# A list schedule takes the order of its choices from a table: runs of instructions with a turn of their own, in a four-layer model on one core

## The chip, the cores and the metric

The kernel runs on one core of a Trainium2 chip. Its time is the device time of one execution in microseconds (us), and lower is better. The engines are named as in the profile: PE (TensorE matmul) and PEld (its weight load), DVE (VectorE), ACT (ScalarE), POOL (GpSimd) and SP (SyncE, which here only issues DMAs).

## The reference

A stack of four layers works on 512 tokens of 1024 features, in float32. Each layer is a mixer and a gated feed-forward block, each with an RMS norm in front and a residual behind; the four mixers differ.

```python
for i in range(DEPTH):                       # 4
    hn = rmsnorm(h, norm_mix[i])
    if t == 0:   m = rwkv7_mix(hn, ...)      # 16 heads, a state of 64x64 per head, a scan over the tokens
    elif t == 1: m = swa_sink_mix(hn, ...)   # attention in a window of 128, 16 query and 2 key heads
    elif t == 2: m = sgu_chunk_mix(hn, ...)  # gelu, a gate that mixes tokens in chunks of 128
    else:        m = gla_mix(hn, ...)        # gated linear attention, 4 heads
    h = h + m
    gate, up = split(rmsnorm(h, norm_ffn[i]) @ ffn_w_in[i])
    h = h + (silu(gate) * up) @ ffn_w_out[i] # hidden size 2816
return rmsnorm(h, norm_final)
```

## The kernel before

Every product in float32 is made of three products in the faster float32r form: both operands are split into a rounded part and a remainder, and `mm3` (L584) issues high times high, high times low and low times high into one PSUM bank. A weight tile goes through three steps: a DMA brings it as `wraw`, ACT copies its rounded part to `whi`, and DVE subtracts that and leaves the remainder in `wlo`. There are 8 `wraw`, 4 `whi` and 4 `wlo` buffers, and 8 PSUM banks, which the program calls `ps`.

The feed-forward blocks and several projections use seven products in place of eight (`seven`, L833, a Strassen-like scheme). Some of its weight operands are sums: the first quarter comes by a DMA that SP issues, and a second DMA, issued by POOL, adds another quarter to the same `wraw` buffer. That buffer is added to only after ACT and DVE have read it for the product before. A feed-forward block has six hidden parts and three output parts, each of seven products. The seven are named m1, m2, m5, m3, m6, m7, m4 in order. The last three are accumulated in the same two banks one after the other, and DVE reads the banks between them: into `slot` tiles in the hidden half (`hidden`, L909), into the residual `h` in the output half (`out_steps`, L819). So m7 can write a bank only when DVE has read m6 from it.

The first mixer has a serial part (`rwkv_chain`, L1325): for each chunk of 64 tokens PE multiplies, ACT copies a result to `vu`, PE multiplies with that (operand `tok`), and DVE makes the next state `st`. While one group of heads goes through its chain, `ahead` (L1105) prepares the next one, with many small steps on ACT (`ew`, `et`) and DVE. The second mixer (`swa`, L1432) projects the queries (`project`, eight tiles of 24 matmuls of 128x512 each), and computes scores for blocks of 128 tokens (`attend`, L1486): matmuls of 128x256 and 128x128 into a bank, which DVE then reads with a mask.

What sets the order of the work is not the order of the program text. All calls are recorded first as 18309 `Op` objects (`record`, L226; the profile gives L234, the line of that helper, for nearly all instructions), with their number `i`, their dependencies, and a cost from a formula (`price`, L264). Then `run` (L290) is a list scheduler: it keeps for each engine the ready instructions in a list sorted by `i`, walks through it, and takes the first one that can start, unless a later one can start over 200 ns (`SLACK`) sooner. Over all engines the candidate that starts first is issued. Only instructions up to 700 (`WINDOW`) behind the first unfinished one are looked at. Each engine then executes its instructions in that order, and waits where one is not ready.

Where the scheduler's own clock sees PE idle for over 450 ns (`GAP`), `keep_warm` (L398) puts in products of the identity matrix with itself, which compute nothing that is used ("fills"; `products`, L493, L496 in the profile), to hold the clock that the hardware grants to TensorE. `ahead_of_cold` (L422) adds some where too little work lies in the last stretch.

Of the kernel before, what the change touches and what calls it, by code (L numbers as in the profile page):

```python
# [28 lines left out]
TABLES = {AF.Exp: "exp", AF.Ln: "ln", AF.Sigmoid: "sigmoid", AF.Tanh: "tanh", AF.Silu: "silu", AF.Gelu: "gelu", AF.Sin: "sin"}  # L29
ALSO = {"exp": ("tanh",), "sigmoid": ("tanh",), "silu": ("sin", "tanh"), "gelu": ("tanh",)}  # L30
ORDER = 1
EARLY = (("pa", 1), ("iv", 4), ("ew", 4))
LATE = (("qk", 4), ("pr", 1), ("et", 11), ("mt", 6), ("tok", 3), ("wu", 2), ("vu", 4), ("out", 5))
VECS = ("norm_mix", "rw_mu", "rw_w0", "rw_a0", "rw_k_k", "rw_k_a", "rw_r_k", "rw_gn_g", "rw_gn_b", "norm_ffn", "sw_b_qkv", "sg_b_u", "gla_b_a",
# [141 lines left out]


class Op:
    __slots__ = ("i", "eng", "call", "deps", "outs", "wait", "cost", "lat", "table", "bufs", "ready", "end", "done", "columns", "form")


class Engine:
# [7 lines left out]
class Program:  # L190
# [99 lines left out]
    def run(self):  # L290
        ops, n = self.ops, len(self.ops)
        for op in ops:
            op.wait = len(op.deps)
            for d in op.deps:
                d.outs.append(op)
            for b in op.bufs:
                b.left += 1
# [3 lines left out]
        dma, table, work = 0.0, None, {}  # L301
        self.work = work
        avail = {e: [] for e in now}
        head, limit = 0, 0
        order = 0
        while order < n:
# [2 lines left out]
            new = min(n, head + self.WINDOW)  # L309
            for op in ops[limit:new]:  # L310
                if op.wait == 0:
                    bisect.insort(avail[op.eng], (op.i, op))
            limit = max(limit, new)
            best = None
            for e, lst in avail.items():
                cand, floor = None, None
                for i, op in lst:
                    s = max(now[e], op.ready)
                    ok = True
                    for b in op.bufs:  # L320
                        if b.held:
                            continue
                        sl = b.pool.slots[b.name]
                        if not sl.may(b, head) or b.psum and b.span[0] > head and len(sl.free) <= self.FREE and not self.soon(b, head):
                            ok = False
                            break
                        s = max(s, min(sl.free) + self.SEM)
                    if not ok:
                        continue
                    if op.table and op.table != table and not (table and op.table in ALSO.get(table, ())):  # L330
                        s += 1300.0
                    if floor is None or s < floor - self.SLACK:
                        if floor is None or s < floor:
                            floor = s
                        cand = (s, i, op)
                    elif s < floor:
                        floor = s
                    if floor <= now[e]:
                        break
                if cand:  # L340

                    if best is None or cand[0] < best[0]:
                        best = cand + (e,)
            if best is None:
                raise RuntimeError("no instruction can go on at %d of %d: %s" % (order, n, [(e, len(l)) for e, l in avail.items()]))
            s, i, op, e = best
            if e == "PE" and self.warm and op.ready > 0.0:
                now["PE"] = self.keep_warm(now["PE"], s, work)
                if now["PE"] > s or self.ahead_of_cold(now, s, op, work):
                    continue  # L350
            avail[e].remove((i, op))
            if op.table and op.table != table and not (table and op.table in ALSO.get(table, ())):
                table = op.table
            cost = op.cost
# [11 lines left out]
            end = s + cost  # L366
# [17 lines left out]
            for o in op.outs:  # L384
                raw = o.deps[op]
                if o.eng == e and e == "PE" or o.eng == "":
                    t = end
                elif o.eng == e:
                    t = (fin if raw else end) if op.lat != 2000.0 else fin
                else:  # L390
                    t = fin if raw else (end + self.SEM if op.lat != 2000.0 else fin)
                o.ready = max(o.ready, t)
                o.wait -= 1
                if o.wait == 0 and o.i < limit:
                    bisect.insort(avail[o.eng], (o.i, o))
        self.time = max(now.values())

    def keep_warm(self, now, s, work):  # L398
# [1624 lines left out]
```

## Time and profile before

| What | Value |
|---|---|
| Time, median of 3 runs | 2528.71 us (2522.41 to 2529.03) |
| Time of the profiled execution | 2518.66 us |
| Its span, first to last instruction | 2516.9 us |
| Mean granted TensorE clock | 0.995 |
| Instructions | 37778, of them 14254 matmul records |
| Read from HBM | 393.95 MB |

The span is what the profile shows; the execution's own time is 1.8 us longer. The profiled execution is 10 us faster than the median of the runs. A float32 matmul leaves two records in the trace, a float32r matmul or a transpose one. The ends of matmuls are modelled, and neighbours overlap in the records. The stages in the trace, by the place of their matmuls: first mixer to 500 us, feed-forward 500 to 840, second mixer 840 to 1009, feed-forward to 1348, third mixer to 1624, feed-forward to 1961, fourth mixer to 2168, feed-forward to the end.

### The profile page before, as it was taken

What the parts mean: (1) busy time and instruction counts of PE and PEld (TensorE: products, weight loads), DVE (VectorE), ACT (ScalarE), POOL (GpSimd) and SP (SyncE); (2) the same over time, 40 slices, a digit from 0 to 9 for tenths busy, and PEclk for the clock granted to TensorE, in tenths of its full rate; (3) what the DMA queues carried; (4) which work ended last, traced back from release to release, by engine and by line L of the source; (5) the groups of instructions that cost most, each with busy time, mean ns of one, the idle gap of its engine ahead of it and who ended that gap; (6) DMA issues with size and microseconds to landing.
All of it is one profiled execution on the core that took longest, in us unless ns stands there. A gap on an engine that the chain in (4) does not pass through costs nothing.

```text
span 2516.9 us, 37778 instructions
## 1 busy us (share of the span) xinstructions
PE 2451.4 (97%) x14254; PEld 2013.8 (80%) x14254; DVE 1935.5 (77%) x3051; ACT 1398.1 (56%) x2269; POOL 406.9 (16%) x456
## 2 busy tenths in 40 slices
PE   9999999999999999999999999999999999999998
PEld 8577778998878766988787788898878888888786
DVE  7684886688778874887779877887768878976868
ACT  4544454465646456756466444665546756755555
POOL 0000000022122232121211300122111221121111
PEclk9999999999999999999999999999999999999999
DMA  5220002389897422898987836699888775889885
GB/s 170 67 69 10 10 4 69 115 199 230 214 229 175 119 85 51 187 219 226 206 212 174 241 101 155 138 216 234 207 214 188 174 184 128 184 205 225 218 200 120
DMA packets 128631, 400.88 MB, mean 159 GB/s; under 512 B 14384, under 2 KB 21040, under 8 KB 128448
## 3 DMA queue, kind: packets, MB, share of 16 engines
q0 software_dynamic: 50688, 171.99, 38.6%
q1 hardware_dynamic: 77760, 226.47, 27.1%
q8 instruction: 112, 1.84, 0.3%
q14 instruction: 71, 0.58, 0.1%
HBM read 393.95 MB, written 2.10 MB: 157 GB/s over the span
## 4 chain that ended last, share of the span: by engine, by line
PE 68%; DVE 11%; DMA 8%; issue 6%; ACT 5%; POOL 1%; SPq 0%; DVEq 0%; POOLq 0%; ACTq 0%
PE ps L234 68%; DMA wraw<-ffn_w_b 4%; DVE slot L234 4%; DVE wlo L234 2%; DMA wraw<-ffn_o_a 2%; ACT slot L234 2%; ACT whi L234 2%; DVE h L234 1%; DVE et L234 1%; DMA wraw<-ffn_o_b 1%; POOL wraw L234 1%; PE ps L496 1%; DVE left L234 1%; POOL slot L234 0%; DVE mt L234 0%
## 5 line engine op out<-in xcount | busy, mean ns | idle before, releaser
L234 PE MATMUL ps<-whi,slot 128*128 128x512 f32 (+1 forms) x4960 | 1529.3, 384 | 17.7 <-DVE slot L234 11.2
L234 PEld LDWEIGHTS ps<-whi,slot 128*128 128x128 f32 x4960 | 921.6, 188 | 196.7 <-issue 20.0
L234 ACT CAST whi<-wraw 128x1024 fp32r<-128x1024 f32 (+3 forms) x680 | 674.9, 997 | 636.5 <-PE ps L234 446.1
L234 DVE TENSOR_TENSOR wlo<-wraw,whi 128x1024 fp32r<-128x1024 f32 (+2 forms) x680 | 786.7, 1165 | 258.4 <-ACT whi L234 255.7
L234 PE MATMUL ps<-wlo,slot 128*128 128x512 f32 (+1 forms) x2480 | 948.1, 383 | 4.3 <-DVE wlo L234 4.0
L234 PEld LDWEIGHTS ps<-wlo,slot 128*128 128x128 f32 x2480 | 466.2, 188 | 85.5 <-DVE wlo L234 8.7
L234 PE MATMUL ps<-slot,whi 128*128 128x512 f32 (+3 forms) x976 | 277.8, 367 | 1.8 <-ACT slot L234 0.9
L234 DVE TENSOR_TENSOR slot<-ps,slot 128x512 f32<-128x512 f32 (+2 forms) x269 | 157.5, 607 | 73.5 <-PE ps L234 57.7
L234 PEld LDWEIGHTS ps<-slot,whi 128*128 128x128 f32 (+2 forms) x976 | 170.4, 184 | 47.2 <-DVE slot L234 8.8
L234 POOL DMA_DIRECT2D wraw<-ffn_w_a x128 | 110.4, 863 | 514.1 <-DVE wlo L234 434.6
L234 DVE TENSOR_TENSOR slot<-left,slot 128x512 fp32r<-128x512 f32 (+1 forms) x250 | 161.0, 662 | 36.3 <-ACT slot L234 30.7
L234 DVE TENSOR_TENSOR h<-h,ps 128x512 f32<-128x512 f32 x240 | 159.2, 684 | 32.1 <-PE ps L234 29.9
L234 PE MATMUL ps<-slot,wlo 128*128 128x512 f32 (+3 forms) x488 | 177.2, 363 | 0.0
L234 ACT CAST slot<-left 128x512 fp32r<-128x512 f32 (+1 forms) x250 | 145.3, 601 | 40.8 <-PE ps L234 26.4
L234 ACT COPY slot<-ps 128x512 f32<-128x512 f32 (+1 forms) x154 | 85.2, 566 | 57.4 <-PE ps L234 54.0
L234 POOL DMA_DIRECT2D wraw<-ffn_w_b x64 | 55.5, 876 | 317.0 <-DMA wraw<-ffn_w_b 95.9
L234 PEld LDWEIGHTS ps<-slot,wlo 128*128 128x128 f32 (+2 forms) x488 | 89.7, 184 | 16.6 <-issue 2.9
L234 POOL DMA_DIRECT2D wraw<-ffn_o_a x64 | 55.2, 862 | 275.2 <-DVE wlo L234 161.6
L234 PE MATMUL ps<-ident,slot 128*128 128x128 f32 (+2 forms) x672 | 89.1, 265 | 1.7 <-DVE slot L234 1.5
L234 PEld LDWEIGHTS ps<-ident,slot 128*128 128x128 f32 (+2 forms) x672 | 69.2, 140 | 26.6 <-issue 5.7
L234 DVE TENSOR_TENSOR slot<-slot 128x512 f32<-128x512 f32 (+7 forms) x131 | 77.5, 611 | 4.2 <-ACT slot L234 2.3
L234 ACT COPY left<-ps 128x512 f32<-128x512 f32 x100 | 50.5, 556 | 53.5 <-PE ps L234 53.4
(281 smaller groups left out, 2299.7 us busy)
## 6 DMA issues: line engine op xcount, KB each, us to landing
wraw<-ffn_w_a SPq DMA_DIRECT2D x128, 512.0 KB, 6.5
wraw<-ffn_w_a POOLq DMA_DIRECT2D x128, 512.0 KB, 6.2
wraw<-ffn_o_a SPq DMA_DIRECT2D x64, 512.0 KB, 5.0
wraw<-ffn_o_a POOLq DMA_DIRECT2D x64, 512.0 KB, 7.8
wraw<-ffn_w_b SPq DMA_DIRECT2D x64, 384.0 KB, 3.6
wraw<-ffn_w_b POOLq DMA_DIRECT2D x64, 384.0 KB, 6.4
wraw<-ffn_o_b SPq DMA_DIRECT2D x16, 512.0 KB, 4.4
wraw<-ffn_o_b POOLq DMA_DIRECT2D x16, 512.0 KB, 8.0
```

What stands on the lines that cost most here:

```text
L234: op = self.add(eng.name, lambda: getattr(eng.target, what)(*map(real, args), **{k: real(a) for k, a in kw.items()}), *self.price(eng.name ...
L496: self.nc.tensor.target.matmul(t, i, i, start=True, stop=True)
```

## The change

Each instruction gets a `turn`, at first its number. A table `TURNS` of 117 rows (first number, end, shift) over all stages moves runs of instructions: their turn is their number plus the shift. The lists of ready instructions are sorted by the turn, and by the number where turns are equal. All else stays: instructions, dependencies, costs, the window of 700 (which still goes by the number), buffers and the rule of the 200 ns.

```diff
+TURNS = (
+    (0, 192, -3283), (192, 384, -2134), (384, 412, -1837), (412, 464, -482), (464, 492, -1382), (536, 588, -2292), (616, 644, 25), (696, 724, -1506),
...
+    (6688, 6717, 14279), (6722, 6751, 3372), (6751, 6758, -290), (6830, 6859, -211), (7118, 7147, 4551), (7154, 7183, -371), (7190, 7219, 12145),
...
+)
...
     def run(self):
         ops, n = self.ops, len(self.ops)
         for op in ops:
+            op.turn = op.i
+        for a, b, t in TURNS:
+            for op in ops[a:b]:
+                op.turn = op.i + t
...
-                    bisect.insort(avail[op.eng], (op.i, op))
+                    bisect.insort(avail[op.eng], (op.turn, op.i, op))
...
-                for i, op in lst:
+                for _, i, op in lst:
...
-            avail[e].remove((i, op))
+            avail[e].remove((op.turn, i, op))
...
-                    bisect.insort(avail[o.eng], (o.i, o))
+                    bisect.insort(avail[o.eng], (o.turn, o.i, o))
```

Some shifts are large: a run with +14279 is last in its list until the window of 700 stops the others, a run with -3283 is first. Others are a few dozen, which puts two neighbouring products of a feed-forward block at nearly the same turn.

The programs differ in two counts: the fills, and the loads of ACT's function tables. Of 142 fills (each a matmul of two records) 98 are left: 57 at the start in both, 43 (in 15 pieces) between 200 and 422 us of the profile of before against 22 (in 6), 10 in the second mixer against none, 14 in other places ahead of 500 us or in the third and fourth mixer against none, and 18 against 19 in the output projection of the first mixer. ACT's table loads go from 22 to 20. All other instructions are the same, in another order. The line numbers grow: L234 becomes L253, and L496 becomes L520.

Three places show how. The first is ACT in the chain of the first mixer, around 225 to 233 us of the profile of before. `vu<-ps` is the copy that the chain waits for, `out` and `tok` belong to the chain too, and `ew` and `et` to the group that is being prepared. Before:

```order
L234 COPY vu<-ps 64x256
L234 ACT_TABLE_LOAD
L234 ACTIVATE ew<-ps,vec 128x512 x4
L234 ACTIVATE et<-ew,ka_1330,vec 128x512 x2
L234 COPY out<-ps 64x256
L234 COPY tok<-ps 128x512
L234 COPY vu<-ps 64x256
```

The same two copies of the chain in the changed program:

```order
L253 COPY vu<-ps 64x256
L253 ACT_TABLE_LOAD
L253 ACTIVATE et<-ew 128x512 x3
L253 COPY out<-ps 64x256
L253 COPY tok<-ps 128x512
L253 COPY vu<-ps 64x256
```

Between one `vu` copy of the chain and the next stood six activations and now stand three; the four of `ew` have moved ahead of the chain.

The second place is PE in the second mixer, at 872 to 881 us. Matmuls of 128x256 and 128x128 are scores, those of 128x512 with `whi` or `wlo` are a projection, and those of L496 are fills. Before:

```order
L234 MATMUL ps<-slot 128x128 x4
L234 MATMUL ps<-slot 128x256 x8
L234 MATMUL ps<-slot 128x128 x2
L234 MATMUL ps<-slot 128x256 x3
L496 MATMUL ps<-ident 128x128 x2
L234 MATMUL ps<-slot 128x256
L496 MATMUL ps<-ident 128x128 x2
L234 MATMUL ps<-slot 128x256 x4
```

The same scores in the changed program:

```order
L253 MATMUL ps<-slot 128x128 x4
L253 MATMUL ps<-slot 128x256 x8
L253 MATMUL ps<-slot,whi 128x512 x2
L253 MATMUL ps<-slot,wlo 128x512
L253 MATMUL ps<-slot,whi 128x512 x2
L253 MATMUL ps<-slot,wlo 128x512
L253 MATMUL ps<-slot,whi 128x512 x2
L253 MATMUL ps<-slot,wlo 128x512
L253 MATMUL ps<-slot,whi 128x512 x2
L253 MATMUL ps<-slot 128x256 x2
```

The scores came in one lump with fills in it, and now are spread between the matmuls of a projection that has been held back.

The third place is PE in the last feed-forward block, at 2382 to 2386 us, with the numbers of the buffers. It is the step from m6 to m7 in an output half: `ps_22204` and `ps_22216` are the two banks that DVE must read in between. Before:

```order
L234 MATMUL ps_22204<-whi_22349,slot_22324 128x512
L234 MATMUL ps_22216<-whi_22349,slot_22297 128x512
L234 MATMUL ps_22216<-wlo_22366,slot_22297 128x512
L234 MATMUL ps_22216<-whi_22349,slot_22324 128x512
L234 MATMUL ps_22216<-whi_22349,slot_22297 128x512
L234 MATMUL ps_22216<-wlo_22366,slot_22297 128x512
L234 MATMUL ps_22216<-whi_22349,slot_22324 128x512
L234 MATMUL ps_22204<-whi_22370,slot_22321 128x512
```

In the changed program the two banks have the numbers 22137 and 22150, and `ps_22356` and `ps_22374` belong to the next hidden product. The first rows of the same step:

```order
L253 MATMUL ps_22137<-whi_22282,slot_22303 128x512
L253 MATMUL ps_22150<-whi_22282,slot_22230 128x512
L253 MATMUL ps_22356<-whi_22300,slot_20461 128x512
L253 MATMUL ps_22150<-wlo_22309,slot_22230 128x512
L253 MATMUL ps_22356<-wlo_22327,slot_20461 128x512
```

After thirteen more rows, the first bank is written again, in the last row here:

```order
L253 MATMUL ps_22150<-whi_22371,slot_22254 128x512
L253 MATMUL ps_22374<-whi_22300,slot_20525 128x512
L253 MATMUL ps_22356<-whi_22341,slot_20510 128x512
L253 MATMUL ps_22356<-wlo_22360,slot_20510 128x512
L253 MATMUL ps_22137<-whi_22371,slot_22254 128x512
```

Between the last write of m6 into the first bank and the first of m7 lay 6 matmuls, and now lie 21, since another product runs mixed with this one. Counted over the whole program, the matmuls of 128x512 and 128x384 in a feed-forward block change the bank that they write 1096 times before and 1917 times now.

More of the change, by code (lines that the diff above doesn't have):

```diff
@@ L178 @@
 class Op:
-    __slots__ = ("i", "eng", "call", "deps", "outs", "wait", "cost", "lat", "table", "bufs", "ready", "end", "done", "columns", "form")
+    __slots__ = ("i", "eng", "call", "deps", "outs", "wait", "cost", "lat", "table", "bufs", "ready", "end", "done", "columns", "form", "turn")
 class Engine:
@@ L292, in run @@
         for op in ops:
+            op.turn = op.i
+        for a, b, t in TURNS:
+            for op in ops[a:b]:
+                op.turn = op.i + t
+        for op in ops:
             op.wait = len(op.deps)
```

15 rows, old and new, of the table TURNS are left out of this document.

## The prediction

> **What bounds the kernel now.** I read the busy times of the engines first, then the chain that ended last, then the stages in windows of time, and last the timeline at the waits.
>
> ```profile
> span 2516.9 us, 37778 instructions
> PE 2451.4 (97%) x14254; PEld 2013.8 (80%) x14254; DVE 1935.5 (77%) x3051; ACT 1398.1 (56%) x2269; POOL 406.9 (16%) x456
> ...
> L234 PE MATMUL ps<-whi,slot 128*128 128x512 f32 (+1 forms) x4960 | 1529.3, 384 | 17.7 <-DVE slot L234 11.2
> ```
>
> TensorE is busy for 97% of the span, so by this row 65.5 us are idle. That is a lower bound for what waiting costs, since one matmul record lasts 384 ns, while in the chain below 316 of them follow each other in 71.05 us, 225 ns apiece: a gap shorter than some 160 ns is hidden behind the record's own modelled end.
>
> ```profile
> 586.68 71.05 PE ps L234 x316
> ...
> 2454.27 51.63 PE ps L234 x232
> ```
>
> The second row says where PE's work ends: at 2505.9 us, 11.0 us before the span does.
>
> The Trainium skill says the same more strongly ("Perfetto Trace Analysis", section Identifying the Most-Contended Engine): matmul busy time is a bad measure of the distance to the limit, and the busy time of the weight loads a good one. By the 80% of the PEld row there would be 503 us of room; no term below uses that, because the 225 ns pitch leaves a reordering nothing to take from a dense stretch.
>
> The stages, in the columns PE, PEld, DVE, ACT and POOL busy, granted clock (PEclk), DMA share and GB/s:
>
> ```profile
> 20.00:200.00 180.00, 176.37 (x1031) 128.24 (x1031) 137.62 (x232) 84.30 (x126) 2.05 (x8) 1.00 0.24 72
> 200.00:422.00 222.00, 210.73 (x2959) 170.39 (x2954) 163.69 (x393) 111.92 (x230) 11.21 (x18) 0.98 0.07 23
> ...
> 500.00:840.00 340.00, 335.56 (x1591) 280.53 (x1591) 278.20 (x376) 201.49 (x290) 72.19 (x80) 1.00 0.88 208
> 840.00:1009.00 169.00, 164.18 (x784) 118.21 (x783) 105.00 (x211) 90.04 (x260) 51.42 (x45) 0.97 0.25 68
> 1009.00:1348.00 339.00, 335.65 (x1598) 281.58 (x1596) 266.72 (x357) 204.48 (x300) 63.41 (x74) 1.00 0.88 209
> 1348.00:1624.00 276.00, 267.64 (x1255) 219.16 (x1254) 228.13 (x346) 137.25 (x196) 40.57 (x40) 1.00 0.65 163
> 1624.00:1961.00 337.00, 334.28 (x1597) 281.16 (x1596) 263.75 (x350) 200.29 (x288) 63.37 (x74) 1.00 0.90 208
> 1961.00:2168.00 207.00, 201.69 (x1137) 167.68 (x1136) 174.66 (x288) 132.30 (x221) 39.25 (x41) 1.00 0.73 164
> 2168.00:2517.00 349.00, 331.39 (x1560) 279.07 (x1558) 265.60 (x371) 192.60 (x271) 60.50 (x70) 0.99 0.82 191
> ```
>
> PE is the bound in every stage, and no other engine is full: DVE has 164 of 222 us in the chain of the first mixer. So the time can only fall by what PE loses to waits, to fills and to a lower clock, and only an order of work can change that. Losses stand in three kinds of places: the chain of the first mixer (200 to 422 us), the second mixer (840 to 1009), and single waits in the feed-forward blocks.
>
> **The change part by part.** No useful instruction is added or removed, so the sum goes by stage. The fills, by the groups of line 496, whole and in the two stages:
>
> ```profile
> L496 PE MATMUL ps<-ident 128*128 128x128 f32 x284 | 42.8, 303 | 3.6 <-DVE slot L234 1.9 <-POOL ident L234 1.4
> ...
> L496 PE MATMUL ps<-ident 128*128 128x128 f32 x86 | 13.8, 299 | 0.1
> ...
> L496 PE MATMUL ps<-ident 128*128 128x128 f32 x20 | 5.5, 426 | 2.1 <-DVE slot L234 1.9
> ```
>
> *First mixer, 200 to 422 us.* PE is idle for 222.00 - 210.73 = 11.3 us, fills take 13.8 us (86 records, 43 fills), and the clock of 0.98 costs 0.02 x 222 = 4.4 us: 29.5 us that are not work. How such a wait arises:
>
> ```profile
> 225.98 1.28 ACT L234 ACT_TABLE_LOAD   x1
> ...
> 227.27 2.43 ACT L234 ACTIVATE ew<-ps,vec 128x512 f32<-128x512 f32 x4
> ...
> 229.57 1.53 ACT L234 ACTIVATE et<-ew,ka,vec 128x512 f32<-128x512 f32 x2
> ...
> 229.95 0.83 PE L496 MATMUL ps<-ident 128*128 128x128 f32 x6
> ...
> 232.12 0.37 ACT L234 COPY vu<-ps 64x256 f32<-64x256 f32 x1
> ...
> 232.54 0.71 PE L234 MATMUL ps<-vu,tok 128*128 128x128 f32 x4 [1.76 <-ACT vu L234]
> ...
> 234.23 1.67 ACT L234 ACTIVATE et<-ew 128x512 f32<-128x512 f32 x3
> ```
>
> ACT works in its own order, and the copy that the chain needs stood behind six activations of the next group (2.43 + 1.53 = 3.96 us); PE did 0.83 us of fills and waited 1.76. In the first place of the new order three activations stand there, 1.67 us by the last row: ACT is free 2.3 us sooner, nearly the 2.6 us of fills and wait. That is one place. For the stretch I go by the fills that the scheduler still puts in, 22 for 43: it fills where its own clock sees PE idle, and by that clock 21 of 43 holes are gone. I let idle time, fills and lost clock shrink alike, by 21/43. Gain 29.5 x 0.49 = 14.4 us; the bounds are 0 (each fill is replaced by idling) and 29.5.
>
> *Second mixer.* Idle 169.00 - 164.18 = 4.8, fills 5.5, clock 0.03 x 169 = 5.1: 15.4 us.
>
> ```profile
> 877.47 1.08 PE L496 MATMUL ps<-ident 128*128 128x128 f32 x4 [0.82 <-DVE slot L234]
> ...
> 879.12 0.69 DVE L234 SCALAR_TENSOR_TENSOR slot<-ps,mask 128x512 f32<-128x512 f32 x1
> ```
>
> Scores come in a lump, and each bank of them must be read by DVE (0.69 us) before the next can be written. In the new order (second place) projection matmuls stand between, 24 x 0.225 = 5.4 us for each tile held back, and the fills here are none. I take two thirds, 10.3 us, and not all, because the last blocks of attention have no projection left to hide behind. Bounds 0 and 15.4.
>
> *Fills elsewhere.* 14 go and one comes, at 42.8 / 142 = 0.30 us each: 3.9 us. If nothing fills their place it is 0.
>
> *Feed-forward blocks.* Their idle time is 4.4, 3.4 and 2.7 us in the first three, and 349.00 - 331.39 - 11.0 = 6.6 in the last: 17.1 us. A clock dip adds to it:
>
> ```profile
> 235.00:250.00 15.00, 14.97 (x113) 11.75 (x112) 12.98 (x26) 4.76 (x11) 0.31 (x1) 0.81 0.07 19
> ...
> 925.00:940.00 15.00, 12.82 (x71) 9.35 (x70) 12.06 (x21) 1.73 (x2) 1.48 (x1) 0.79 0.32 83
> 2220.00:2230.00 10.00, 7.51 (x37) 6.93 (x35) 5.40 (x8) 5.03 (x8) 0.00 (x0) 0.83 0.49 138
> 2381.00:2386.00 5.00, 2.48 (x12) 1.78 (x11) 4.19 (x5) 1.93 (x3) 0.00 (x0) 1.00 0.97 278
> ```
>
> That is 0.17 x 10 = 1.7 us in the row at 2220. The two longest waits:
>
> ```profile
> 2223.56 0.44 PE L234 MATMUL ps<-whi,slot 128*128 128x384 f32 x1 [2.49 <-DVE slot L234]
> ...
> 2382.56 1.05 ACT L234 CAST whi<-wraw 128x1024 fp32r<-128x1024 f32 x1 [1.43 <-DMA wraw<-ffn_o_a]
> ...
> 2383.64 1.23 DVE L234 TENSOR_TENSOR wlo<-wraw,whi 128x1024 fp32r<-128x1024 f32 x1 [0.65 <-ACT whi L234]
> 2384.78 1.28 DVE L234 TENSOR_TENSOR h<-h,ps 128x512 f32<-128x512 f32 x2
> 2385.61 0.47 PE L234 MATMUL ps<-whi,slot 128*128 128x512 f32 x1 [2.52 <-DVE h L234]
> ```
>
> The lower four rows are one cause: weights land late, so ACT's copy and DVE's `wlo` are late, and the reading of the bank that PE waits for is queued behind that `wlo` on DVE. In the new order (third place) 21 matmuls lie between m6 and m7 where 6 lay; 15 more at 0.225 us are 3.4 us, over the 2.52. Of the 17.1 us I take two thirds, 11.4, since some steps still run unmixed, and the dip with it: 13.1 us, bounds 0 and 18.8. For the third and fourth mixer (8.4 + 5.3 us idle) I take nothing.
>
> *ACT's tables.* Two loads less spare ACT 2 x 1.28 us. It is busy for 56% of the span, and where it does hold PE up the chain's term above has it, so I count nothing more.
>
> *What is new.* Two products mixed hold two pairs of the four `whi` and `wlo` buffers, so a weight tile is prepared with less lead, and DVE's queue decides more often. The price of one miss is a `wlo` pass, 1.23 us by the row above; I take five, 6.2 us. The bounds are 0 and the rival below.
>
> Sum: 14.4 + 10.3 + 3.9 + 13.1 - 6.2 = 35.5 us. The profiled execution took 2518.66 us, 1.8 more than its span, so the changed one would take 2483 in such an execution. The runs shown have their median 10 us higher, at 2528.71; on that scale it is 2493 us. A measurement of this kernel can tell about 0.3%, 7.6 us, from no change.
>
> **The rivals.** *More goes than I take* (chance 0.10): all of the first three terms and of the feed-forward, 29.5 + 15.4 + 3.9 + 18.8 = 67.6 us, gives 2461. For it: the fills show that the scheduler sees few holes left. Against it: 17.1 us of idling in feed-forward stages had hardly a fill, so its clock doesn't see them all.
>
> *The holes stay, only empty* (0.10): a fill stands where PE has nothing ready. If the chains on ACT and DVE are as long as before, PE idles in place of the fills, and the few waits won are paid back by new ones: 2529. For it: DVE is busy for 164 of 222 us in the chain, so a copy moved forward pushes another back. Against it: the two first places put real work there, not nothing.
>
> *The clock* (0.05): fills are there to hold it, and nine of the fifteen pieces of fills between 200 and 422 us go. If each of the nine brings a dip like that at 235 us, 0.19 x 15 = 2.9 us, that is 26 us, and 2519 are left: 0.4% faster. Against it: fills stood in the dips at 235 and 925 us and did not prevent them. The Trainium skill has the rule ("TensorE: Matmul & The Clock Gate", Part 1): after an idle window of about 3.4 us the array runs at half rate. By that rule, single holes well below 3.4 us bring no dip; the trace is divided on it, with a clock of 1.00 around the wait of 2.52 us at 2385 and of 0.83 around that of 2.49 us at 2224.
>
> *Weights come late* (0.09), on the other side: the feed-forward windows have a DMA share of 0.88 to 0.90, and mixed products ask for the loads of two at once from the same 8 `wraw` buffers. Each late landing ahead of a bank's reading costs 2.5 us, as at 2224 and 2385. Seventeen of them eat the 41.7 us that the other terms give; with 20, one in 13 of the 252 products of the four blocks, the time is 2537. For it: such waits exist, and DMA is fullest there. Against it: a buffer is added to for a later product, and mixing puts more PE time between the two uses, as in the third place.
>
> **How the numbers follow.** The main case has 0.66, with 20 to 50 us gained: 2479 to 2509, 2493 the likeliest. The range goes on to the case of more at 2461 and to no change at 2529, which leaves out the late weights, half of the empty holes, and the tail beyond 2461. Faster by over 0.3%: 0.66 + 0.10 + 0.03 of the clock = 0.79; within: 0.10 + 0.02 = 0.12; slower: 0.09.
>
> **What would show it.** Right: between 200 and 422 us of before the stage takes about 14 us less and the second mixer about 10; at the m6 to m7 step of the last block no wait of 2.5 us is left; PE idle falls from 65.5 to some 45 us. Wrong: stages of the same length with PE busy lower (empty holes), a granted clock of 0.95 or less in the first mixer (clock), or feed-forward stages longer than 340 us with waits of ACT for `wraw` (late weights).

## The result and the profile after

The changed kernel takes 2466.68 us, the median of 4 runs (2461.81 to 2470.02). The kernel before, run beside it, takes 2526.2 us (4 runs, 2522.41 to 2529.03). The ratio is 0.9764, with an interval from 0.9738 to 0.979: 59.5 us less by the medians. The profiled execution of the changed kernel took 2470.02 us, near the top of its runs, and that of before was near the bottom of its own, so the two traces differ by less: 2516.9 - 2468.3 = 48.6 us of span. What follows about stages explains these 48.6 us.

The head of the page of the changed kernel, with the group of plain matmuls:

```profile
span 2468.3 us, 37524 instructions
PE 2411.1 (98%) x14166; PEld 1995.9 (81%) x14166; DVE 1930.5 (78%) x3051; ACT 1389.3 (56%) x2267; POOL 400.2 (16%) x456
...
L253 PE MATMUL ps<-whi,slot 128*128 128x512 f32 (+1 forms) x4960 | 1509.7, 385 | 13.7 <-DVE slot L253 7.4
```

PE's idle time went from 65.5 to 2468.3 - 2411.1 = 57.2 us, which is little. Its busy time fell by 40.3 us, although every useful matmul is still there. So most of the gain lies inside what the profile calls busy: fills, clock, and matmuls that follow each other more closely.

The stages of the changed kernel, in windows, with the columns of the prediction's table (PE, PEld, DVE, ACT and POOL busy, granted clock, DMA share, GB/s). The first mixer ends at 474 us, the others are at 815 to 971, 1310 to 1577 and 1921 to 2128 us, and the feed-forward blocks lie between and behind them:

```profile
20.00:200.00 180.00, 179.88 (x1065) 134.37 (x1066) 139.85 (x236) 87.90 (x132) 1.64 (x6) 1.00 0.23 74
200.00:400.00 200.00, 191.10 (x2910) 156.01 (x2906) 162.14 (x391) 103.33 (x222) 10.72 (x19) 1.00 0.09 28
...
474.00:815.00 341.00, 333.83 (x1581) 280.93 (x1579) 274.53 (x373) 198.26 (x284) 71.53 (x79) 0.99 0.87 206
815.00:971.00 156.00, 150.85 (x768) 111.50 (x767) 105.19 (x212) 90.30 (x261) 49.21 (x45) 1.00 0.26 73
971.00:1310.00 339.00, 334.77 (x1595) 283.73 (x1594) 266.02 (x357) 202.98 (x300) 62.05 (x74) 0.99 0.89 209
1310.00:1577.00 267.00, 265.47 (x1244) 218.35 (x1242) 224.50 (x345) 138.64 (x196) 38.54 (x38) 1.00 0.66 164
1577.00:1921.00 344.00, 335.09 (x1590) 281.59 (x1589) 263.43 (x350) 198.42 (x288) 62.73 (x75) 1.00 0.86 205
1921.00:2128.00 207.00, 201.44 (x1138) 167.91 (x1137) 175.89 (x291) 133.57 (x223) 40.27 (x42) 1.00 0.73 165
2128.00:2468.30 340.30, 329.03 (x1560) 277.59 (x1558) 265.27 (x370) 191.19 (x270) 60.56 (x70) 0.99 0.85 198
```

The first three mixers are shorter, and all four are at full clock; the fourth is as long as before. In the second mixer 156.00 - 150.85 = 5.15 us are idle, and there is no fill: what was 15.4 us of waits, fills and lost clock is 5.15. In the third mixer the idle time went from 8.4 to 1.5 us. The feed-forward blocks are idle longer than before: 7.2, 4.2, 8.9 and, in the last one, 340.3 - 329.0 less a tail of 10.3 us, 1.0: 21.3 us against 17.1.

What PE waited for, longest sums first (total us, times, longest us), in the changed kernel and then in before:

```profile
PE ps L253 <- DVE slot L253: 20.1, 15, 3.5
PE ps L253 <- DVE wlo L253: 4.1, 6, 1.2
PE ps L253 <- DVE h L253: 3.8, 4, 1.1
...
PE ps L253 <- ACT vu L253: 0.9, 1, 0.9
```

```profile
PE ps L234 <- DVE slot L234: 17.3, 25, 2.5
PE ps L234 <- DVE h L234: 9.6, 9, 2.5
PE ps L234 <- ACT vu L234: 4.8, 7, 1.9
```

The wait for the chain's `vu` copy is nearly gone (4.8 to 0.9 us), and so are the waits for `h`: none of them is over 1.1 us, so the 2.52 us at the step from m6 to m7 are gone. The waits for `slot` are fewer and longer; the longest, 3.5 us, is in a feed-forward block.

For every traced execution I also added up the distances from one PE record to the next by the stage to which the matmul belongs (fills go to the stage of the next useful matmul). This table is used throughout; times are in us. The tail is from the start of PE's last record to the end of the span:

| Execution | 1st mixer | FFN 1 | 2nd | FFN 2 | 3rd | FFN 3 | 4th | FFN 4 | tail | span |
|---|---|---|---|---|---|---|---|---|---|---|
| before | 497.2 | 339.6 | 170.3 | 338.0 | 276.5 | 336.4 | 207.8 | 338.1 | 11.4 | 2516.9 |
| changed | 470.3 | 342.3 | 156.8 | 338.0 | 268.0 | 344.4 | 206.2 | 330.5 | 10.3 | 2468.3 |
| e1, first mixer's rows | 469.6 | 341.7 | 177.2 | 341.9 | 274.5 | 339.6 | 209.7 | 332.5 | 11.5 | 2499.5 |
| e2, no FFN rows | 469.5 | 341.0 | 157.6 | 341.4 | 268.6 | 336.8 | 206.4 | 335.0 | 11.4 | 2469.1 |
| e3, FFN rows only | 497.3 | 341.0 | 171.0 | 337.0 | 274.0 | 343.1 | 210.9 | 330.6 | 10.2 | 2516.6 |
| e4, before, no later fills | 498.4 | 340.1 | 169.5 | 344.1 | 275.8 | 336.7 | 210.5 | 334.5 | 11.4 | 2522.5 |
| e6, second mixer's rows | 496.4 | 341.3 | 159.3 | 341.3 | 277.2 | 337.9 | 209.1 | 335.4 | 11.5 | 2510.9 |
| e7, third and fourth | 496.6 | 340.7 | 171.0 | 341.0 | 268.9 | 336.2 | 207.3 | 332.9 | 11.7 | 2507.8 |
| e8, changed, no later fills | 467.5 | 344.2 | 160.4 | 339.2 | 266.7 | 342.1 | 210.0 | 330.0 | 10.2 | 2471.6 |
| e9, changed, small adds | 469.5 | 334.0 | 156.8 | 332.1 | 266.0 | 332.3 | 204.7 | 328.3 | 10.3 | 2435.5 |
| e10, before, small adds | 496.0 | 338.6 | 168.9 | 336.5 | 273.3 | 335.2 | 206.5 | 331.5 | 11.4 | 2499.4 |
| e11, front rows only | 486.6 | 344.9 | 169.0 | 340.4 | 275.7 | 337.5 | 207.8 | 335.1 | 11.4 | 2509.8 |
| e12, changed, FFN 3 as before | 470.1 | 342.8 | 158.0 | 336.2 | 269.1 | 338.6 | 208.2 | 329.3 | 10.3 | 2464.0 |

The first mixer is the same to 2 us wherever its order is the same. A feed-forward block differs by up to 6 us from execution to execution of one order (the second one in before's order: 338.0 to 344.1). The second mixer in before's order took 168.9 to 171.0 us, but 177.2 in e1; the fourth took 206.5 to 210.9. So only the first mixer may be read from one trace, and a difference of a few us in the others only from several.

### The profile page after: what moved, and what is told of

It is laid out like the page before. It is cut to its first block, busy times and chain, and to the rows that moved or that the text cites. A ratio compares the mean times of both kernels' runs of the same rounds, so it can differ in the third digit from the quotient of the medians.

```text
span 2468.3 us, 37524 instructions
## 1 busy us (share of the span) xinstructions
PE 2411.1 (98%) x14166; PEld 1995.9 (81%) x14166; DVE 1930.5 (78%) x3051; ACT 1389.3 (56%) x2267; POOL 400.2 (16%) x456
## 4 chain that ended last, share of the span: by engine, by line
PE 71%; DMA 9%; DVE 9%; ACT 5%; issue 4%; POOL 1%; SPq 0%; DVEq 0%; POOLq 0%; ACTq 0%
PE ps L253 71%; DMA wraw<-ffn_w_a 3%; DMA wraw<-ffn_w_b 2%; DVE wlo L253 2%; ACT slot L253 2%; DVE slot L253 2%; DMA wraw<-ffn_o_a 2%; ACT whi L253 1%; DVE h L253 1%; POOL wraw L253 1%; DVE et L253 1%; DMA wraw<-sg_w_v 1%; DVE mt L253 0%; DMA wraw<-gla_w_qk 0%; POOL slot L253 0%
## 5 line engine op out<-in xcount | busy, mean ns | idle before, releaser
L253 PE MATMUL ps<-whi,slot 128*128 128x512 f32 (+1 forms) x4960 | 1509.7, 385 | 13.7 <-DVE slot L253 7.4
L253 PEld LDWEIGHTS ps<-whi,slot 128*128 128x128 f32 x4960 | 923.4, 188 | 186.2 <-DVE slot L253 14.7
L253 ACT CAST whi<-wraw 128x1024 fp32r<-128x1024 f32 (+2 forms) x680 | 673.8, 997 | 619.5 <-PE ps L253 426.6
L253 DVE TENSOR_TENSOR wlo<-wraw,whi 128x1024 fp32r<-128x1024 f32 (+2 forms) x680 | 783.7, 1161 | 237.9 <-ACT whi L253 233.8
L253 PE MATMUL ps<-wlo,slot 128*128 128x512 f32 (+1 forms) x2480 | 932.7, 383 | 4.1 <-DVE wlo L253 4.1
L253 PEld LDWEIGHTS ps<-wlo,slot 128*128 128x128 f32 x2480 | 466.8, 188 | 85.7 <-DVE wlo L253 7.9
L253 PE MATMUL ps<-slot,whi 128*128 128x512 f32 (+3 forms) x976 | 276.1, 366 | 1.8 <-ACT slot L253 0.9
L253 DVE TENSOR_TENSOR slot<-ps,slot 128x512 f32<-128x512 f32 (+2 forms) x269 | 159.0, 607 | 79.7 <-PE ps L253 70.6
L253 PEld LDWEIGHTS ps<-slot,whi 128*128 128x128 f32 (+2 forms) x976 | 170.4, 184 | 40.4 <-issue 4.5
L253 POOL DMA_DIRECT2D wraw<-ffn_w_a x128 | 111.0, 879 | 483.2 <-DVE wlo L253 339.4
L253 DVE TENSOR_TENSOR h<-h,ps 128x512 f32<-128x512 f32 x240 | 159.0, 684 | 26.6 <-PE ps L253 24.3
L253 DVE TENSOR_TENSOR slot<-left,slot 128x512 fp32r<-128x512 f32 x250 | 160.2, 662 | 23.5 <-ACT slot L253 15.4
L253 PE MATMUL ps<-slot,wlo 128*128 128x512 f32 (+3 forms) x488 | 176.5, 366 | 0.0
L253 ACT CAST slot<-left 128x512 fp32r<-128x512 f32 (+1 forms) x250 | 143.4, 601 | 29.0 <-PE ps L253 18.0
L253 ACT COPY slot<-ps 128x512 f32<-128x512 f32 (+2 forms) x154 | 85.3, 566 | 72.4 <-PE ps L253 66.0
L253 PEld LDWEIGHTS ps<-slot,wlo 128*128 128x128 f32 (+2 forms) x488 | 89.5, 184 | 18.4 <-issue 3.7
L253 POOL DMA_DIRECT2D wraw<-ffn_o_a x64 | 55.9, 873 | 297.3 <-DVE wlo L253 210.5
L253 POOL DMA_DIRECT2D wraw<-ffn_w_b x64 | 55.1, 867 | 300.2 <-DVE wlo L253 99.4
L253 PE MATMUL ps<-ident,slot 128*128 128x128 f32 (+2 forms) x672 | 88.8, 265 | 6.6 <-DVE slot L253 6.4
L253 PEld LDWEIGHTS ps<-ident,slot 128*128 128x128 f32 (+2 forms) x672 | 68.8, 140 | 31.1 <-DVE slot L253 10.6
L253 DVE TENSOR_TENSOR slot<-slot 128x512 fp32r<-128x512 f32 (+7 forms) x131 | 77.2, 611 | 12.1 <-DMA slot<-slot 7.2
L253 ACT COPY left<-ps 128x512 f32<-128x512 f32 x100 | 51.0, 555 | 44.1 <-PE ps L253 44.0
```

The lines of the kernel that those rows point to most:

```text
L253: op = self.add(eng.name, lambda: getattr(eng.target, what)(*map(real, args), **{k: real(a) for k, a in kw.items()}), *self.price(eng.name ...
```

## The experiments

**One part of the table at a time.** In e1, e2, e3, e6, e7, e11 and e12 the changed kernel goes through only some rows of `TURNS`; the steps without rows keep their numbers. The edit is one line, here that of e1; the other conditions are on `r[0]` as well:

```diff
-        for a, b, t in TURNS:
+        for a, b, t in [r for r in TURNS if r[0] < 4159]:
```

*e1, the first mixer alone.*

> Only the rows of the table that belong to the first mixer are applied; all later stages keep the order of before. If the first mixer is where most of the time went (its end came 25 us sooner in the trace of after), the time is 24 to 30 us under before, near 2499 us. If the gain is spread over the stages by their length, a fifth of it falls here: some 12 us, near 2514 us.

Measured: 2502.41 us against 2523.99, ratio 0.9922 (0.9899 to 0.9944). That is 21.6 us less, short of the 24 to 30 expected. By the table the first mixer falls from 497.2 to 469.6 us, as in the changed kernel. It is the largest single part, and more than the 14.4 us that the prediction gave to its chain.

*e2, without the rows of the feed-forward blocks, and e3, with only these.*

> The rows of the four feed-forward blocks are left out, the rows of the four mixers stay. If mixing two products in the feed-forward blocks wins nothing net (their stages together were 3 us longer in the trace of after), the time is that of after or up to 5 us less: 2460 to 2467 us. If the feed-forward rows win the 7 us that the prediction gave them net, this is 7 us slower than after, near 2474 us.

> Only the rows of the four feed-forward blocks are applied. If mixing wins nothing net, the time is that of before or up to 5 us more: 2525 to 2531 us. If it wins what the prediction said, 7 us less: near 2519 us.

Measured: e2 2471.96 us, ratio 0.9805 (0.9779 to 0.983); e3 2518.1 us, ratio 0.9979 (0.9965 to 0.9993). The rows of the feed-forward blocks are worth 5.9 us by e3, and 5.3 us by the medians of e2 and the changed kernel, whose intervals overlap (by their ratios it is 0.0041, some 10 us). In the traces they are worth nothing: the four blocks sum to 1352.1 us in before and 1351.7 in e3, and over all executions with whole weights to 1350.8 to 1357.9 in before's order and 1351.7 to 1355.5 in the new one. My theory after the result, that mixing wins nothing, does not hold by the times, if only just; that it wins little does.

*e6, the second mixer alone, and e7, the third and the fourth.*

> Only the rows of the table for the second mixer. The prediction takes 10.3 us there and 3 us of fills with it; the profiles of before and after have 13.5 us between their stages. Both give 2510 to 2513 where before has 2524. If the stage is only shorter in the changed program because the block ahead of it leaves more loaded weights or a fuller queue, the gain is under 6 us: 2518 or more.

> Only the rows of the table for the third and the fourth mixer. The prediction takes nothing there but 3 us of fills: 2521 where before has 2524. The profiles have 8.5 and 1.6 us between their stages: 2514. If these 10 us are what the block ahead hands over, or chance of one execution, the time is 2521 to 2524.

Measured: e6 2511.3 us against 2523.43, ratio 0.995 (0.9932 to 0.9968); e7 2514.02 us, ratio 0.9961 (0.9944 to 0.9977). In e6 the second mixer takes 159.3 us instead of 170.3. In e7 the third takes 268.9 instead of 276.5, and the fourth 207.3 instead of 207.8. So the gain of the third mixer is its own, and the prediction had nothing there beside its five fills. With e1 and e3 the four parts add up to 7.8 + 5.0 + 3.9 + 2.1 = 18.8 thousandths. The whole table gives 23.6. The gap of 4.8 is at the edge of what the intervals allow (taken together, 3.6 for the four parts and 2.6 for the whole), so it stays open whether the parts simply add up or help each other.

**The fills.** In e4 the kernel before, and in e8 the changed one, counts the fills behind the first 57 without issuing them; both edits are the same in `keep_warm` and `ahead_of_cold`:

```diff
-            call(n)
+            call(n) if self.fills < 57 else None
...
-        call(n)
+        call(n) if self.fills < 57 else None
```

> The kernel before in its own order, without the 85 fills behind the first 57; the fills compute nothing that is used. If a fill stands where PE has to wait anyway, nothing is won: within 6 us of before. If a fill costs its 0.30 us, 25 us are won, near 2501 us. If the fills hold the clock, the granted clock falls below the 0.995 of before and the time rises by 10 us or more.

> The changed kernel without the 41 fills behind the first 57. Theory: fills stand in holes, cost nothing and hold little, as they did in before without its fills: 2467, within 5 us of the changed kernel, at a granted clock of 0.99. The clock rival: with the fills gone the clock drops to half for windows of 3.4 us around each of the 8 pieces of fills, 8 x 1.7 = 14 us at most, 2480. A gain of over 7 us would say that fills delay the work that they stand before.

Measured: e4 2518.63 us, ratio 0.9987 (0.997 to 1.0004), no difference, at a mean clock of 0.989 for 0.995. The windows of e4 for the first and the second mixer:

```profile
200.00:422.00 222.00, 204.85 (x2832) 162.61 (x2828) 160.93 (x382) 108.88 (x222) 11.62 (x19) 0.95 0.06 21
842.00:1010.00 168.00, 162.79 (x764) 116.72 (x763) 105.04 (x210) 89.89 (x260) 51.13 (x45) 0.96 0.25 68
```

Between 200 and 422 us of e4, PE is idle for 17.2 us and 0.05 x 222 = 11.1 us go to the clock: 28.3 us that are not work, where before has 11.3 of idling, 13.8 of fills and 4.4 of clock, 29.5. The 43 fills there bought 6.7 us of clock and covered 5.9 us of idling, for 13.8 us of their own; it comes out even, within the 1 us or so that the rounding of each clock column leaves. That is the rival of the empty holes in its pure form: who only takes the fills away gains nothing. In the changed kernel it is the waits that went, and the fills with them: without later fills in either kernel the new order still brings 2518.63 - 2472.53 = 46.1 us, by e4 and e8.

Measured for e8: 2472.53 us against 2523.43, ratio 0.9813 (0.9794 to 0.9831), clock 0.993. By the medians it is 5.9 us slower than the changed kernel, and the two intervals just miss each other. But the table shows nothing of it in the first mixer, where all of these fills were (467.5 for 470.3 us); the second and the fourth mixer, which have no fills in either, were 3.6 and 3.8 us longer in this one trace. So the 5.9 us, a little over the 5 expected, stay without a cause. The clock rival's 14 us are not there.

**The shape of the matmuls.** The shape of a matmul here is that of the operand that is loaded as weights, rows by columns. After the result I found that PE's order changes it 321 times for 369, and, counted ahead of useful matmuls alone, 265 for 298 in the first mixer. e5 measures such a change by itself, in the kernel before, with products of the identity behind the first fills:

```diff
+            mm = self.nc.tensor.target.matmul
+            a = lambda: mm(t, i, i, start=True, stop=True)
+            b = lambda: mm(t[:64, :64], i[:64, :64], i[:64, :64], start=True, stop=True)
+            c = lambda: mm(t, i[:64], i[:64], start=True, stop=True)
+            c2 = lambda: mm(other, i[64:], i[64:], start=True, stop=True)
+            if self.nc.fills == 0:
+                other = self.ps.tile_pool.tile([P, S], F32, name="ps")[:, :P]
+                for run in ([a] * 100, [b] * 100, [a, b] * 100, [a, a, b, b] * 50, [c] * 100, [c, c2] * 50, [a, c] * 100):
+                    for f in run:
+                        f()
```

> The kernel before, with 1000 products of the identity matrix added behind the first fills, in seven runs: 100 of 128x128 by 128x128 (a), 100 of 64x64 by 64x64 (b), 100 pairs a b, 50 times a a b b, 100 of 64x128 by 64x128 (c), 50 pairs of c in the two halves of the array's rows, and 100 pairs a c. Theory: the part of the first mixer's gain that the prediction had no term for (6.9 us of matmul time for the same matmuls at the same clock) comes from fewer changes of the matmul's shape, 33 of 298. A change then costs about 0.1 us by the traces' pitch (112 ns from record to record of one shape, 205 at a change), so a b alternating takes some 20 us longer than a and b in two blocks, a a b b some 10 us. Second part of it: neighbours in different halves of the rows overlap, so c alternating between the halves takes clearly less than c in one half (the changed order has 20 more of these neighbours). Rival: shapes cost nothing, and the pitch of 205 ns was a wait; then all runs last the sum of their parts, to 2 us.

The seven runs as windows of e5's trace, from the first record of each to the first of the next (length, PE busy with its records, and so on):

```profile
9.99:32.41 22.42, 22.42 (x202) 22.30 (x200) 1.19 (x5) 3.40 (x6) 0.30 (x1) 1.00 0.43 160
32.41:44.22 11.81, 11.81 (x202) 11.74 (x201) 0.00 (x0) 0.00 (x0) 0.00 (x0) 1.00 0.01 1
44.22:111.55 67.33, 67.33 (x402) 48.52 (x401) 0.00 (x0) 0.00 (x0) 0.00 (x0) 1.00 0.00 1
111.55:162.22 50.67, 50.67 (x403) 41.29 (x401) 0.00 (x0) 0.00 (x0) 0.00 (x0) 1.00 0.00 1
162.22:184.54 22.32, 22.32 (x202) 22.32 (x201) 0.00 (x0) 0.00 (x0) 0.00 (x0) 1.00 0.00 1
184.54:195.91 11.37, 11.37 (x204) 11.25 (x202) 0.00 (x0) 0.00 (x0) 0.00 (x0) 1.00 0.01 3
195.91:279.24 83.33, 83.33 (x401) 59.19 (x400) 0.00 (x0) 0.00 (x0) 0.00 (x0) 1.00 0.00 1
```

A hundred a and a hundred b in blocks take 22.42 + 11.81 = 34.2 us; in turn, with 200 changes, 67.33. A change costs 33.1 / 200 = 0.166 us. With half the changes (a a b b) it is 50.67, again 0.164 us each. Between a and c it is (83.33 - 44.7) / 200 = 0.193 us. All of it counts as busy time: the windows are busy from end to end. In the runs of a and b the trace shows why the cost is higher than the 0.1 us expected: not only is the record at the change late (205 and 148 ns behind the last, where 112 and 58 are usual), the one behind it is too (107 and 213 ns). And c in alternate halves of the rows takes 11.37 us for 100, half of the 22.32 in one half. A change of shape has its price, nearly twice what I had expected; the rival, that shapes cost nothing, is out.

The Trainium skill has the rule behind it ("TensorEngine Tiling (Array Packing)", section Tiling Modes): changing the tiling mode, and not just the tile, drains the array, while different tiles work in parallel. It gives no price there; this trace agrees, at 0.16 to 0.19 us a change and with the halves of the rows side by side.

*e11, the front of the first mixer alone*, the rows ahead of number 1166.

> Only the first eleven rows of the table, those for the projections ahead of 153 us of the first mixer; the chain keeps its numbers. By the account of the two profiles the front loses 3.5 us of idle time and four fills, 4.6 us: 2519 where before has 2524. If the front's rows are what lets the chain start sooner and run closer, most of the first mixer's 20 us come with them: 2510 or less. If the chain's rows carry all of it: 2524.

Measured: 2509.6 us against 2521.14, ratio 0.9956 (0.9942 to 0.997). The first mixer takes 486.6 us for 497.2. So these eleven rows bring 10.6 of the first mixer's 26.9 us, more than the 4.6 that I expected. The price of shapes, which I had not put in, can make up most of that: PE's order has 278 changes for 298, and 20 x 0.166 to 0.193 us are 3.3 to 3.9 us. That leaves some 2 us open, which is what the first mixer differs by between executions. The time of 2509.6 is that of "2510 or less", but the kernel before ran at 2521.14 beside it; by the stage neither "most of it comes with the front" nor "the chain's rows carry all of it" is true. The other 16.3 us are left for the chain's rows.

**Late weights.** In e9 (the changed kernel) and e10 (before) an accumulating DMA moves only the first quarter of its columns, so both kernels leave out part of the sums of weights; the order of the instructions on PE is the same:

```diff
-(*map(real, args), **{k: real(a)
+(*[real(x)[:, :x.shape[1] // 4] if "accum_op" in kw else real(x) for x in args], **{k: real(a)
```

> The changed kernel with each accumulating DMA moving only the first quarter of its columns, in the same order of instructions; it leaves out three quarters of the sums of weights that a feed-forward block adds up in its buffers. Theory of late weights: PE is idle for some 21 us in the four feed-forward blocks of the changed kernel (7.2 + 4.2 + 8.9 and 1 us), because accumulated weights land late (ACT waits 42.3 us for wraw, before 11.8 in that group); with a quarter of the bytes the waits of ACT go and the blocks take 8 to 15 us less: 2452 to 2459 where the changed kernel has 2467. Rival: the waits come from the order on DVE and ACT, and DMA has room; then the time stays within 3 us.

> The same in the kernel before, as the control. If late weights cost it less than the changed kernel, as the rival of the prediction has it (mixed products ask for the loads of two at once), it gains less than the changed one with the same edit: 0 to 5 us, 2519 to 2524. If it gains as much or more, the mixing has not made weights later.

Measured: e9 2436.81 us, ratio 0.9667 (0.9648 to 0.9687); e10 2501.28 us against 2521.14, ratio 0.9926 (0.9901 to 0.995). So late landings cost both kernels more than I expected: the changed one 0.0097 x 2521 = 24 us and before 19 by the ratios, 29.9 and 19.9 by the medians. The intervals, 2 to 2.6 thousandths each, leave open by the times whether the changed one loses more. In the traces it does: its four blocks take 28.5 us less with small adds, those of before 10.3. The feed-forward windows, first of e9, then of e10:

```profile
474.00:807.00 333.00, 331.26 (x1583) 280.11 (x1582) 274.40 (x371) 198.50 (x286) 71.54 (x79) 1.00 0.53 135
963.00:1295.00 332.00, 331.74 (x1587) 281.02 (x1586) 265.02 (x356) 201.71 (x297) 61.99 (x74) 1.00 0.54 136
1560.00:1894.00 334.00, 333.90 (x1608) 282.57 (x1607) 265.04 (x353) 200.96 (x292) 62.94 (x75) 1.00 0.53 135
2097.00:2435.50 338.50, 328.47 (x1562) 278.12 (x1560) 265.01 (x371) 191.56 (x271) 60.56 (x70) 0.99 0.49 123
```

```profile
500.00:838.00 338.00, 334.40 (x1585) 279.40 (x1584) 276.75 (x373) 200.25 (x287) 71.79 (x80) 1.00 0.52 133
1005.00:1343.00 338.00, 335.93 (x1600) 281.93 (x1599) 266.73 (x357) 204.53 (x301) 63.39 (x74) 1.00 0.53 135
1615.00:1951.00 336.00, 334.26 (x1597) 281.20 (x1595) 263.44 (x351) 200.39 (x289) 63.48 (x74) 1.00 0.51 133
2157.00:2499.40 342.40, 329.69 (x1560) 277.62 (x1558) 265.12 (x371) 192.60 (x271) 60.51 (x70) 0.99 0.47 121
```

With the DMA share at about half, where it was 0.82 to 0.90, PE's idle time in the four blocks falls from 21.3 to 2.1 us in the changed kernel (1.74 + 0.26 + 0.10 and nothing in the last, less the tail) and from 17.1 to 8.7 in before (3.60 + 2.07 + 1.74 + 1.3). Where weights come in time, mixing the products wins 1341.8 - 1326.7 = 15.1 us by the sums of the table. Where they come late, the same order wins some 6 us by e3. ACT does not wait longer for the weights in sum: its waits for those of the feed-forward blocks are 102.7 us in the trace of before (76 waits, the longest 3.3 us) and 98.2 in the changed kernel (53, the longest 5.2). They are fewer and longer (the 42.3 and 11.8 us of the expectation are one group of four), and more of their time reaches PE: 21.3 - 2.1 = 19.2 us of its idling go with the small adds, and 8.4 in before. How a late landing stops the changed kernel, in its first feed-forward block:

```profile
601.99 1.99 ACT L253 CAST whi<-wraw 128x1024 fp32r<-128x1024 f32 x2 [5.17 <-DMA wraw<-ffn_w_a]
603.07 1.22 DVE L253 TENSOR_TENSOR wlo<-wraw,whi 128x1024 fp32r<-128x1024 f32 x1 [3.66 <-ACT whi L253]
604.21 0.74 DVE L253 SCALAR_TENSOR_TENSOR slot<-slot,ncol 128x512 f32<-128x512 f32 x1
...
605.01 0.55 PE L253 MATMUL ps<-ident,slot 128*128 128x128 f32 x3 [3.50 <-DVE slot L253]
```

ACT waits 5.17 us for the weights, DVE stands with `wlo` behind ACT, and the step that PE needs, `slot`, stands on DVE behind that `wlo`, though by its operands, `slot` and `ncol`, it reads no weights. PE waits 3.50 us.

**A version that beats both?** In e12 the third feed-forward block, which took longer mixed in every trace with whole weights, keeps the order of before.

> The changed kernel without the table's rows for the third feed-forward block (1577 to 1921 us of its profile), which keeps the order of before; a try for a version that beats both. In every traced execution with these rows that block took 342 to 344 us, in every one without them 336 to 340; the last block, mixed too, took 330 to 331 against 333 to 338. Theory of late weights: whether mixing wins depends on what the block's loads find, and here it loses about 5 us: 2462 where the changed kernel has 2467, ratio 0.9745. Rival: the blocks' differences are chance of single executions, or the 5 us come back in the block behind: 2467, ratio 0.9764.

Measured: 2459.87 us against 2520.13 (5 runs, 2456.88 to 2465.74), ratio 0.9753 (0.9727 to 0.978). The block takes 338.6 us for 344.4, as expected, and the median is the lowest of all with the whole of the computation. But the ratio of the changed kernel, 0.9764, lies inside the interval: that it beats it stays open.

## Why the prediction was right, and where it was not

The sign, the range and the main reason held: waits on PE in the mixers went, fills and clock losses with them, at no cost elsewhere that eats it. The gain was put too low: 35.5 us for 59.5 by the medians or 48.6 by the spans. The measured 2466.68 us lies outside the main case, 2479 to 2509, and inside the range only because that went on to 2461. The list scheduler's own clock was nearer: `self.time` at the end of `run`, an estimate of the program and no measurement, is 2482.5 us for the kernel before and 2421.2 for the changed one, 61.2 less. By the prediction's own terms, against the spans:

- **First mixer, 14.4 us, measured 26.9.** The whole stage, ahead of and in the chain, in before and in the changed kernel, with its fills:

```profile
20.00:500.00 480.00, 464.71 (x4630) 370.70 (x4630) 343.82 (x726) 230.72 (x434) 15.16 (x27) 0.99 0.18 54
...
L496 PE MATMUL ps<-ident 128*128 128x128 f32 x130 | 19.2, 291 | 0.1
```

```profile
20.00:474.00 454.00, 444.98 (x4584) 359.25 (x4585) 346.47 (x731) 227.18 (x435) 14.27 (x27) 1.00 0.18 58
...
L520 PE MATMUL ps<-ident 128*128 128x128 f32 x82 | 10.8, 279 | 0.0
L520 PE MATMUL ps<-ident 128*128 128x128 f32 x44 | 6.2, 282 | 0.0
```

  (The last row is for 200 to 400 us alone.) The stretch that the term was for went from 29.5 us of no work to 8.9 idle + 6.2 of fills + 0 of clock = 15.1: 14.4 us, exactly the term. That it is exact is luck: idling, fills and clock did not shrink alike, as the term had it, but by 2.4, 7.6 and 4.4 us.

  Over the whole stage, 480 - 454 = 26 us went: 6.3 of idling (15.3 to 9.0), 8.4 of fills, 4.4 of clock, and 6.9 of useful matmuls. (The clock column is rounded; in the window of 234 to 241 us, the only one in the stage below full clock, it is 0.51, which makes 0.49 x 7 = 3.4 us of clock and 7.9 of matmuls.)

  These last are what the prediction had no term for. 33 fewer changes of shape at 0.166 to 0.193 us are 5.5 to 6.4 us, and 12 more neighbours of the shape 64x128 that lie in different halves of the rows, at (22.32 - 11.37) / 100 = 0.11 us each, 1.3. That sum, 6.8 to 7.7, is worked out from e5 and the order, not tried alone in the mixer. The mixer's own traces bear out the larger part: with idle time and the half clock taken off, the distances from record to record at a change and right behind it are, in sum, 46.7 us above the usual ones of their shape in before and 40.6 in the changed kernel (40.7 in e1), 6.1 less.

  The step that failed is the sentence that the 225 ns pitch leaves a reordering nothing to take from a dense stretch, and with it the one that the time can only fall by waits, fills and clock. The first is nearly true of a run of one shape, as in the rows it was read from: between two matmuls of 128x512 in the first mixer, distances over 250 ns went from 34 to 20, and what they had above 227 ns from 3.8 to 2.0 us. It is false where shapes mix. The price could have been read in the kernel: its scheduler adds 92 ns for a change of shape (`TURN`, L357 of the kernel before) and takes 0.56 of the cost for a neighbour in the other half (L359).
- **Second mixer, 10.3 us, measured 13.5.** The 15.4 us of no work fell to 5.15, by 10.25: the term. Here too the size was a guess, two thirds. Of the other 3.3 us four changes of shape make 0.7; the rest is open.
- **Third and fourth mixer, nothing but 3 us of fills, measured 8.5 + 1.6.** The third lost 6.8 us of idle time (8.4 to 1.5) and 1.5 of fills. I had taken nothing because I had read no wait there in the timeline; the idle row was in the table all the same. The fourth's 1.6 is less than it differs by between executions.
- **Feed-forward, 13.1 - 6.2 = 6.9 us, measured 5.9 by e3 and -3.1 in the two traces.** Near by the times. Mixing is worth 15.1 us where no weight is late (13.1 was taken). The new waits take 28.5 - 10.3 = 18.2 us of it in the traces, three times the 6.2 that was taken, and some 5 to 10 by the times of e9 and e10, which the 6.2 fits. They are not five `wlo` passes of 1.23 us: the one shown above cost PE 3.50 us. Idle time went up there and not down, which is why PE's idle time is 57.2 us and not the 45 that I had named.
- **Fills, 3.9 us.** By e4 a fill costs nothing by itself, so this was no term of its own; it belongs to the waits that went.

Of the rivals, "more goes than I take" with its 2461 us comes nearest in time, though not by its mechanism: it wanted all the feed-forward idling gone. "The holes stay, only empty" is what e4 did and the change did not. "Weights come late" is real, at 5 to 18 us and not the 50 of its 20 misses; its sign, feed-forward stages over 340 us with ACT waiting for `wraw`, is there, at 341 and 344 us, but it is not a sharp one, since blocks in before's order took up to 344.9 us too (e11). "The clock" did not come in the mixers. Three windows of the changed kernel, behind the wait of 3.50 us at 605, behind one of 2.19 us that ends at 1014, and in the chain:

```profile
605.00:610.00 5.00, 4.99 (x19) 4.10 (x20) 3.10 (x4) 2.82 (x5) 0.00 (x0) 0.66 0.75 235
1015.00:1020.00 5.00, 5.00 (x22) 4.76 (x21) 2.83 (x5) 2.72 (x4) 1.70 (x2) 0.66 0.92 174
225.00:240.00 15.00, 14.18 (x141) 10.85 (x139) 14.40 (x34) 4.79 (x11) 0.00 (x0) 1.00 0.07 19
```

A dip follows the long wait: 0.34 x 5 = 1.7 us, on top of the 3.50. The same dip follows the wait of 2.19 us, and a third one, again 0.66 over 5 us, the wait of 1.95 us that ends at 1721, while behind the wait of 2.32 us that ends at 1631 us the clock is 1.00. In the chain the short waits that are left bring none. The Trainium skill's rule ("TensorE: Matmul & The Clock Gate", Part 1) is half rate after at least one idle window of about 3.4 us. It agrees with the dip at 605 and with the chain, but the dips behind 2.19 and 1.95 us show that a shorter wait can be enough here.

## What to carry to other kernels

Where a resource is busy for 97% of the time, most of what an order can still win may lie inside the busy time: count fills, clock, and changes of the matmul's shape, and not only gaps. Price every stage's idle row, also where the timeline shows no single long wait. Before mixing two streams to cover waits, see whether their loads land in time; shrinking the transfers, in an experiment, tells how much of the gain waits for them. Where a scheduler with a cost model makes the order, read its prices, and the time at which its own clock ends for both orders, before you price anything by hand.

## What the runs showed of the hardware

- A change between matmuls of 128x128 and 64x64 (float32) costs 0.166 us, between 128x128 and 64x128 0.193 us, and shows as busy time.
- Two matmuls of 64 rows in different halves of the array run side by side: 100 took 11.37 us, and 22.32 in one half.
- Behind waits of PE of 3.50, 2.19 and 1.95 us the granted clock fell to 0.66 over 5 us, 1.7 us each time; behind one of 2.32 us it stayed at 1.00.
- Fills that held the clock at 0.98 where it would have been 0.95 cost as much as they brought (29.5 and 28.3 us of no work).
- A feed-forward block of one and the same order differed by up to 6 us between executions, with a DMA share of 0.82 to 0.90; the first mixer, at 0.18, by 2 us.
